# Which block of a feed-forward network goes through the down projection alone: the last instead of the first

## The chip, the core and the metric

The kernel runs on one core of a Trainium2 chip. The metric is device time in microseconds for the whole program, from one launch. Lower is better. The engines are called as in the profile: PE does the matrix products (PEld its weight loads), DVE elementwise work on two operands, ACT copies and activations, SP issues the loads.

## What is computed

Two token groups (512 and 256 rows of 1024 features) go through a trunk of two layers with shared weights, all in float32. Each layer is a half-weighted SwiGLU network, a mixer (gated and windowed attention in layer 0, neighbourhood attention in layer 1), and a second SwiGLU network. So there are four feed-forward networks ("networks 1 to 4" below), with a mixer between 1 and 2 and one between 3 and 4. The change touches these four alone:

```python
D_MODEL, D_FF = 1024, 2816

def swiglu(h, wg, wu, wd):
    return (jax.nn.silu(h @ wg) * (h @ wu)) @ wd

def odd_layer(x, f1_n, f1_g, f1_u, f1_d, mix_n, w_qkv, rpb, w_out, f2_n, f2_g, f2_u, f2_d):
    x = x + 0.5 * swiglu(rmsnorm(x, f1_n), f1_g, f1_u, f1_d)
    x = x + mixer_c(rmsnorm(x, mix_n), w_qkv, rpb, w_out)
    x = x + 0.5 * swiglu(rmsnorm(x, f2_n), f2_g, f2_u, f2_d)
    return x
```

## The kernel before

The activations lie transposed: features on the partitions, the 768 tokens of both groups along the row, cut into two halves of 384. Float32 is made from two parts of the type fp32r: every weight tile is split into a high part (`whi`, an ACT cast, L114) and the rest (`wlo`, a DVE subtraction, L115), every operand likewise (L196, L197), and one product is three matmuls of 128x384 (`mm3`, L176 to L181). The `w` pool has five buffers for `whi` and five for `wlo`, the `raw` pool four buffers of 512 KB for weights as they come from memory.

**A network** has 2816 = 11 x 256 hidden features, hence 11 "pairs" of 128-wide blocks, numbered 0 to 10. Gate, up and down projections of a pair are each a 2x2 block product that is done with seven products in place of eight, over sums and differences of the blocks. Sums of weights (`s1` to `s4`) are DVE operations at L609, 128x512 each; sums of operands are made once per network for the input (`b11`, `b21`, `t1`, `t2`, `t3`, `n4`, `b22`).

- *Pairs 0 to 3* are "early" (`EARLY = 4`). Their products with `b11` and `b21` are made ahead in the order `ORDER`, while the second token half is still being normalised. What is left of an early pair is p6, p7, p4, p5, p3 (L579): 5 products for gate and 5 for up, 120 matmuls. It begins with p6, whose weights are the sum `s2` times `t2`.
- *Pairs 4 to 9* run p1, p6, p2, p7, p5, p3, p4: 168 matmuls, and begin with p1, whose weights come straight from memory. Pair 10 has an order of its own that begins with p1 as well.
- `keep` (L494, ACT) copies a finished PSUM bank out as `u2` or `u3`, `add` (L499, DVE) adds the second product, `hidden` (L508 to L511) makes the scaled silu(gate) * up.
- While pair p runs, the operands of pair p-1's down projection are made (`operands`, 7 splits and 4 differences, 11 DVE operations). Of these the last six (`operands_2`) are put off into the following down projection where L445 says so.

**Down projections** of pairs 0 to 8 are made by `down` (L629), for two pairs at once or for one. It loads two rows of weights for each pair (L636), makes four sums for each, and runs seven products: 24 matmuls each for two pairs, 12 for one. Four PSUM banks a product are added to `acc` (tiles `p10` to `p13`) or into x by DVE (L661, four adds a product, five products); only in the call that holds pair 0 is `acc` copied by ACT (L659) and not added. ACT copies two sets of banks (L655). Pairs 9 and 10 are left to `down_last`; `last_operands` (L690) adds `acc` into x during pair 10.

PE runs in the order in which the program is written. The order on DVE, ACT and SP is chosen by the framework's list scheduler when the program is built, from priorities and from its own durations; buffers are given out by the same scheduler. On the chip each engine then takes its instructions in that fixed order, with semaphore waits.

In network 1, loads of the weights (L99) share SP's queue with 60 small transfers that build bias tables in memory (`skew`, L1402; `tab`, L1407), one after each weight load.

The calls of `down` are made in the loop at L587 to L593, which the change edits.

Of the kernel before, what the change touches and what calls it, by code (L numbers as in the profile page):

```python
# [20 lines left out]
NPAIR = FF // (2 * P)  # L21
# [30 lines left out]
class Trunk:  # L52
# [364 lines left out]
    def ffn(self, pre):  # L417
# [7 lines left out]
        acc = []  # L425
        d, dl = {}, {}

        def operands(q):


            h = hs.pop(q)
            sub = lambda o, x, y: nc.vector.tensor_tensor(out=o, in0=x, in1=y, op=ALU.subtract)
            d[q] = {}

            def put(n, src):
                d[q][n] = self.dtile(n), self.dtile(n)
                self.split(*d[q][n], src)

            h11, h12, h21, h22 = h[0, 0], h[0, 1], h[1, 0], h[1, 1]
            yield put("b11", h11)  # L440
            yield sub(h11, h12, h11)
            yield put("t1", h11)
            yield put("b21", h21)
            yield sub(h11, h22, h11)
            if q and q % 2 == 0:  # L445
                self.later = operands_2(h, sub, put)
                return
            for _ in operands_2(h, sub, put):
                yield

        def operands_2(h, sub, put):
            h11, h12, h21, h22 = h[0, 0], h[0, 1], h[1, 0], h[1, 1]
            yield put("t2", h11)
            yield sub(h12, h22, h12)
            yield put("t3", h12)
            yield put("b22", h22)
            yield sub(h21, h21, h11)
            yield put("n4", h21)

        def pair(p):  # L460
# [114 lines left out]
            if p:  # L575
                steps = operands(p - 1) if p < NPAIR - 1 else self.last_operands(dl, 0, hs[p - 1], acc)
# [10 lines left out]
        for p in range(NPAIR):  # L587
            for _ in stages[p]:
                pass
            if p == 1:  # L590
                acc += [self.fw.tile([P, H], F32, tag=f"p1{j}", name=f"p1{j}") for j in range(4)]
            if p % 2 and p < NPAIR - 1:
                self.down(pre, range(max(p - 2, 0), p), d, acc)  # L593
        kind = self.following[0]
        self.norm_begin(self.following)
        if kind == "f":
# [968 lines left out]
```

## Time and profile before

| what | us |
|---|---|
| median of three runs (2632.23 to 2636.09) | 2633.43 |
| the profiled execution, its own time | 2634.87 |
| its span, first to last instruction | 2633.1 |
| PE busy in it, 15094 matmuls | 2561.3 |
| DVE busy, 4793 instructions | 2267.8 |
| ACT busy, 2851 instructions | 1365.6 |

The mean granted clock of PE is 0.99. Three runs lie within 0.15% of each other. A busy PE says little by itself, because the matmuls overlap: one takes 0.33 us in the records and the next starts 0.17 us later. What counts is the start of one matmul against the start of the one before.

Where each network stands in the span, by the first matmul of pair 0's remaining products and the last of `down_last`: network 1 from 60.5 to 518.7, network 2 from 810.7 to 1267.2, network 3 from 1303.0 to 1759.4, network 4 from 2159.4 to 2617.5.

### The profile page before, as it was taken

Reading aid. Unit: us, or ns where it says so; the run is one execution under the profiler, and the core shown is the slowest. Engines: PE = TensorE matmul, PEld = TensorE weight load, DVE = VectorE, ACT = ScalarE, POOL = GpSimd, SP = SyncE. Lnnn points to the kernel's source line nnn. Section 1 sums busy time; section 2 is a strip of 40 time slices with the busy share of each in tenths; the row PEclk is TensorE's granted clock in tenths of the full one; section 3 lists DMA queues with packets and bytes.
Section 4 is the critical chain, followed back from the end, with each engine's and each line's share of the span. In section 5 each row is a group of like instructions: output and inputs, shape, how many; then the busy total and the mean of one; then the engine's idle time right before and its main releaser. Section 6 shows DMA issues by size and latency. Waiting matters only on the chain.

```text
span 2633.1 us, 41175 instructions
## 1 busy us (share of the span) xinstructions
PE 2561.3 (97%) x15094; PEld 2491.3 (95%) x15094; DVE 2267.8 (86%) x4793; ACT 1365.6 (52%) x2851; POOL 88.0 (3%) x172
## 2 busy tenths in 40 slices
PE   7999999998999999999999999999999999999997
PEld 7999999987899999999999999989998989999997
DVE  8998889889779988898999888886777699988886
ACT  7544444555655544454654544454545465454443
POOL 0000000000100000000000000001222100000000
PEclk9999999999999999999999999999999999999998
DMA  5423222421223222222322222232221332222221
GB/s 168 133 78 103 71 81 65 145 87 37 89 77 97 81 81 77 68 75 86 96 81 81 73 73 74 88 111 63 63 63 40 105 104 81 81 71 74 68 87 54
DMA packets 83898, 218.99 MB, mean 83 GB/s; under 512 B 20080, under 2 KB 32880, under 8 KB 83696
## 3 DMA queue, kind: packets, MB, share of 16 engines
q1 hardware_dynamic: 83552, 216.34, 26.5%
q8 instruction: 118, 1.93, 0.3%
q14 instruction: 84, 0.69, 0.1%
q10 hardware_dynamic: 144, 0.03, 0.0%
HBM read 206.90 MB, written 15.07 MB: 84 GB/s over the span
## 4 chain that ended last, share of the span: by engine, by line
PE 86%; DVE 9%; ACT 2%; DMA 2%; issue 1%; SPq 0%; DVEq 0%; ACTq 0%
PE ps_mm L140 54%; PE ps_aux L140 31%; DMA raw<-in_w 1%; DVE wlo L115 1%; PE ps_aux L144 1%; DVE s L609 1%; DVE xl L739 1%; ACT p L911 1%; DVE p L920 0%; DVE p L905 0%; DVE tl L197 0%; ACT whi L114 0%; ACT xh L738 0%; DVE ol L197 0%; DVE x L706 0%
## 5 line engine op out<-in xcount | busy, mean ns | idle before, releaser
L114 ACT CAST whi<-s 128x512 fp32r<-128x512 f32 x496 | 304.9, 621 | 390.6 <-DVE s L609 133.1
L114 ACT CAST whi<-raw 128x512 fp32r<-128x512 f32 x512 | 311.0, 619 | 257.8 <-PE ps_mm L140 116.8
L115 DVE TENSOR_TENSOR wlo<-s,whi 128x512 fp32r<-128x512 f32 x496 | 337.0, 685 | 61.1 <-ACT whi L114 60.8
L115 DVE TENSOR_TENSOR wlo<-raw,whi 128x512 fp32r<-128x512 f32 x494 | 337.5, 691 | 28.3 <-ACT whi L114 24.1
L140 PE MATMUL ps_aux<-dt,whi 128*128 128x384 f32 x864 | 219.3, 334 | 2.1 <-ACT whi L114 2.1
L140 PE MATMUL ps_mm<-db,whi 128*128 128x384 f32 x864 | 219.2, 334 | 0.0
L140 PEld LDWEIGHTS ps_aux<-dt,whi 128*128 128x128 f32 x864 | 156.0, 188 | 2.4 <-ACT whi L114 2.4
L140 PEld LDWEIGHTS ps_mm<-db,whi 128*128 128x128 f32 x864 | 156.1, 188 | 0.0
L140 PE MATMUL ps_mm<-xh,whi 128*128 128x512 f32 (+1 forms) x416 | 147.4, 354 | 3.8 <-ACT xh L738 3.8
L140 PE MATMUL ps_aux<-dt,wlo 128*128 128x384 f32 x432 | 144.4, 334 | 0.3 <-DVE wlo L115 0.3
L140 PE MATMUL ps_mm<-db,wlo 128*128 128x384 f32 x432 | 144.4, 334 | 0.0
L140 PE MATMUL ps_mm<-xl,whi 128*128 128x512 f32 (+1 forms) x416 | 142.3, 342 | 1.1 <-DVE xl L739 1.1
L140 PE MATMUL ps_mm<-xh,wlo 128*128 128x512 f32 (+1 forms) x416 | 142.1, 341 | 0.0
L609 DVE TENSOR_TENSOR s<-raw 128x512 f32<-128x512 f32 x124 | 85.0, 686 | 23.0 <-DMA raw<-in_w 22.9
L499 DVE TENSOR_TENSOR u<-ps_aux,u 128x384 f32<-128x384 f32 x176 | 97.0, 551 | 2.8 <-PE ps_aux L140 2.6
L609 DVE TENSOR_TENSOR s<-raw,raw 128x512 f32<-128x512 f32 x124 | 83.7, 686 | 18.2 <-DMA raw<-in_w 18.0
L140 PE MATMUL ps_aux<-dh,whi 128*128 128x384 f32 x384 | 97.6, 335 | 0.6 <-DVE x L706 0.6
L911 ACT ACTIVATE p<-p,st 128x256 f32<-128x256 f32 (+3 forms) x144 | 68.9, 480 | 55.0 <-DVE st L909 54.9
L494 ACT COPY u<-ps_mm 128x384 f32<-128x384 f32 x176 | 83.5, 474 | 24.2 <-PE ps_mm L140 24.0
L661 DVE TENSOR_TENSOR x<-ps_aux,x 128x384 f32<-128x384 f32 x160 | 86.0, 552 | 9.3 <-PE ps_aux L140 9.2
L140 PEld LDWEIGHTS ps_mm<-xh,whi 128*128 128x128 f32 x416 | 79.9, 192 | 14.1 <-ACT xh L738 4.9
L140 PE MATMUL ps_mm<-oh,whi 128*128 128x384 f32 x256 | 88.1, 344 | 4.6 <-DVE x L888 4.0
(486 smaller groups left out, 8058.2 us busy)
## 6 DMA issues: line engine op xcount, KB each, us to landing
raw<-in_w SPq DMA_DIRECT2D x350, 512.0 KB, 3.7
xdm<-x SPq DMA_DIRECT2D x16, 384.0 KB, 2.3
x<-in_x SPq DMA_DIRECT2D x16, 192.0 KB, 5.5
x<-xdm SPq DMA_DIRECT2D x8, 384.0 KB, 3.4
xold<-xdm SPq DMA_DIRECT2D x8, 384.0 KB, 3.0
out_y<-y SPq DMA_DIRECT2D x8, 384.0 KB, 2.4
tab<-skew SPq DMA_DIRECT2D x8, 256.0 KB, 4.8
raw<-in_w SPq DMA_DIRECT2D x8, 256.0 KB, 2.6
```

The costliest lines, as they stand in the source:

```text
L114: nc.scalar.copy(hi, src)
L115: (eng or nc.gpsimd).tensor_tensor(out=lo, in0=src, in1=hi.bitcast(F32), op=ALU.subtract)
L140: self.nc.tensor.matmul(out, lhsT=lhsT, rhs=rhs, start=start, stop=stop, **kw)
L144: self.nc.tensor.transpose(out, src, self.ident)
L494: nc.scalar.copy(e[n, out], bank[key, n])
L499: nc.vector.tensor_tensor(out=t, in0=bank[key, n], in1=t, op=ALU.add)
L609: f = lambda o, x, y, op: self.nc.vector.tensor_tensor(out=o, in0=x, in1=y, op=op)
L661: nc.vector.tensor_tensor(out=o, in0=ps, in1=o, op=ALU.add)
L739: nc.vector.scalar_tensor_tensor(out=lo, in0=src, scalar=gain, in1=hi.bitcast(F32), op0=ALU.mult, op1=ALU.subtract)
L911: nc.scalar.activation(outs[i], outs[i], AF.Exp, bias=nm[:, i : i + 1], accum_out=sm[:, i : i + 1])
```

## The change

Pairs 0 to 8 are nine, so one of them goes alone. Before, it was pair 0, right after pair 1; then (1,2) after pair 3, (3,4) after pair 5, (5,6) after 7 and (7,8) after 9. Now (0,1) goes after pair 2, (2,3) after 4, (4,5) after 6, (6,7) after 8, and pair 8 alone after pair 9, just before pair 10. The operands that are put off are those of the second pair of each two: before of pairs 2, 4, 6, 8, now of 1, 3, 5, 7.

```diff
@@ operands @@
             yield sub(h11, h22, h11)
-            if q and q % 2 == 0:
+            if q % 2:
                 self.later = operands_2(h, sub, put)
                 return
@@ ffn @@
-            if p == 1:
+            if p == 2:
                 acc += [self.fw.tile([P, H], F32, tag=f"p1{j}", name=f"p1{j}") for j in range(4)]
-            if p % 2 and p < NPAIR - 1:
-                self.down(pre, range(max(p - 2, 0), p), d, acc)
+            if p and p % 2 == 0 and p < NPAIR - 1:
+                self.down(pre, range(p - 2, p), d, acc)
+            if p == NPAIR - 2:
+                self.down(pre, range(p - 1, p), d, acc)
```

The numbers of matmuls, DVE and ACT data operations and loads are the same in both; the lines behind L593 move down by two (L661 becomes L663). In the two mixers the order on DVE and ACT is the same in both kernels. In the networks it is the same in long stretches, with another pair in the same place, and differs most at two places: where the single down projection was, and where it is now.

**ACT at the start of pair 2, network 1.** `whi` is the high part of a weight, `u2` the copy of a finished bank, `db`, `dt`, `dn` operands of the down projection. Before, behind the single down projection:

```order
L516 COPY ps_mm80_1359<-p1_515 128x384
L516 COPY ps_mm82_1387<-p1_537 128x384
L516 COPY ps_mm94_1609<-p1_568 128x384
L516 COPY ps_mm96_1637<-p1_589 128x384
L494 COPY u2_1381<-ps_mm80_1359 128x384
L196 CAST db11_1383<-sg_539 128x384
L114 CAST whi83_1393<-s2_1391 128x512
```

Now, right behind pair 1:

```order
L114 CAST whi58_1192<-s2_1190 128x512
L196 CAST dt3_1117<-u2_726 128x384
L196 CAST db22_1143<-u3_772 128x384
L196 CAST dn4_1170<-sg_842 128x384
L509 ACTIVATE u3_1007<-u3_1007 128x384
L114 CAST whi60_1220<-s2_1218 128x512
L509 ACTIVATE u2_958<-u2_958 128x384
L114 CAST whi61_1241<-s3_1239 128x512
L494 COPY u2_1208<-ps_mm57_1186 128x384
```

Before, the weights of the "up" product with `t2` (`whi83`) stand behind the copy of the finished "gate" product (`u2`); now the same weights (`whi60`) stand four places ahead of that copy.

**DVE at the same place.** Before, the sum `s2` for "up" of pair 2 (`s2_1391`) comes behind the last adds into x of the single down projection:

```order
L661 TENSOR_TENSOR x4_101<-ps_aux64_1220,x4_101 128x384
L661 TENSOR_TENSOR x5_102<-ps_aux66_1226,x5_102 128x384
L661 TENSOR_TENSOR x6_103<-ps_aux68_1232,x6_103 128x384
L661 TENSOR_TENSOR x7_104<-ps_aux70_1238,x7_104 128x384
L609 TENSOR_TENSOR s1_1389<-raw21_1356 128x512
L609 TENSOR_TENSOR s2_1363<-raw18_1347,s2_1363 128x512
L609 TENSOR_TENSOR s2_1391<-s1_1389,raw20_1353 128x512
L609 TENSOR_TENSOR s3_1412<-raw18_1347,raw19_1350 128x512
L197 TENSOR_TENSOR db11_1384<-sg_539,db11_1383 128x384
L115 TENSOR_TENSOR wlo83_1394<-s2_1391,whi83_1393 128x512
```

Now the first down projection is that of pairs 0 and 1, behind pair 2, and ahead of pair 3 DVE has:

```order
L663 TENSOR_TENSOR x3_100<-ps_mm94_1601,x3_100 128x384
L611 TENSOR_TENSOR s1_1764<-raw27_1731 128x512
L663 TENSOR_TENSOR x4_101<-ps_aux80_1485,x4_101 128x384
L611 TENSOR_TENSOR s2_1766<-s1_1764,raw26_1728 128x512
L663 TENSOR_TENSOR x5_102<-ps_aux82_1494,x5_102 128x384
L663 TENSOR_TENSOR x6_103<-ps_aux84_1503,x6_103 128x384
L115 TENSOR_TENSOR wlo104_1769<-s2_1766,whi104_1768 128x512
L663 TENSOR_TENSOR x7_104<-ps_aux86_1512,x7_104 128x384
```

The sum for "up" (`s2_1766`) stands between the adds of the last product and not behind them.

**DVE between the last `down` and pair 10, network 2.** Before, with pairs 7 and 8 in that call, the adds into x stand mixed with the weights (`wlo`) and sums (`s1`, `s2`, `s3`) of pair 10:

```order
L661 TENSOR_TENSOR x3_7712<-ps_mm921_13095,x3_7712 128x384
L115 TENSOR_TENSOR wlo932_13245<-raw170_13220,whi932_13244 128x512
L661 TENSOR_TENSOR x4_7718<-ps_aux907_12979,x4_7718 128x384
L115 TENSOR_TENSOR wlo934_13267<-s2_13264,whi934_13266 128x512
L661 TENSOR_TENSOR x5_7724<-ps_aux909_12988,x5_7724 128x384
L661 TENSOR_TENSOR x6_8190<-ps_aux911_12997,x6_8190 128x384
L609 TENSOR_TENSOR s1_13288<-raw171_13222 128x512
L661 TENSOR_TENSOR x7_8196<-ps_aux913_13006,x7_8196 128x384
L609 TENSOR_TENSOR s2_13290<-s1_13288,raw170_13220 128x512
L609 TENSOR_TENSOR s3_13349<-raw168_13216,raw169_13218 128x512
```

Now pair 8 alone is in that call. Ahead of its last adds stand the weights of pair 10's first product, `wlo929` for gate and `wlo932` for up:

```order
L115 TENSOR_TENSOR wlo926_13177<-s2_13055,whi926_13176 128x512
L115 TENSOR_TENSOR wlo927_13197<-raw167_13051,whi927_13196 128x512
L115 TENSOR_TENSOR wlo929_13226<-raw168_13216,whi929_13225 128x512
L115 TENSOR_TENSOR wlo932_13245<-raw170_13220,whi932_13244 128x512
L663 TENSOR_TENSOR x4_7718<-ps_aux912_13089,x4_7718 128x384
```

Eight adds later (x5 to x7, x0 to x3, and x4 once more) DVE has:

```order
L663 TENSOR_TENSOR x5_7724<-ps_aux914_13095,x5_7724 128x384
L663 TENSOR_TENSOR x6_8190<-ps_aux916_13101,x6_8190 128x384
L663 TENSOR_TENSOR x7_8196<-ps_aux918_13107,x7_8196 128x384
L611 TENSOR_TENSOR s2_13264<-s1_13262,raw168_13216 128x512
L611 TENSOR_TENSOR s1_13288<-raw171_13222 128x512
L692 TENSOR_TENSOR x0_7694<-x0_7694,p10_9713 128x384
L115 TENSOR_TENSOR wlo934_13267<-s2_13264,whi934_13266 128x512
L611 TENSOR_TENSOR s2_13290<-s1_13288,raw170_13220 128x512
L611 TENSOR_TENSOR s3_13349<-raw168_13216,raw169_13218 128x512
```

The twelve adds of pair 8's last three products follow each other, with no weight or sum between them; the sums for pair 10's second product (`s2`) come behind the last of them, the weights of its first product ahead of the first.

## The prediction

> **What bounds the kernel now.** First the page: engines and the chain of work that ended last.
>
> ```profile
> PE 2561.3 (97%) x15094; PEld 2491.3 (95%) x15094; DVE 2267.8 (86%) x4793; ACT 1365.6 (52%) x2851; POOL 88.0 (3%) x172
> ...
> PE 86%; DVE 9%; ACT 2%; DMA 2%; issue 1%; SPq 0%; DVEq 0%; ACTq 0%
> ```
>
> The end is set by PE. PE's work is the same in both kernels, so only the time in which PE stands still or runs slowly can change. Where is it? I cut the networks into stages, each from the first matmul of a pair or a down projection to the first of the next. First undisturbed stages: pair 9, the double down projection of pairs 7 and 8, and pair 10 of network 2 (columns: the stretch, its length, busy time of each engine, granted clock, DMA).
>
> ```profile
> core 0: us, PE busy (x) PEld busy (x) DVE busy (x) ACT busy (x) POOL busy (x), PEclk, DMA share, GB/s
> 1145.69:1174.81 29.12, 29.12 (x169) 29.12 (x169) 26.09 (x48) 13.86 (x29) 0.00 (x0) 1.00 0.24 73
> 1174.81:1203.93 29.12, 29.12 (x169) 29.12 (x169) 26.79 (x51) 12.85 (x26) 0.00 (x0) 1.00 0.24 73
> 1203.93:1233.05 29.12, 29.12 (x169) 29.12 (x169) 25.88 (x48) 17.43 (x34) 0.00 (x0) 1.00 0.41 128
> ```
>
> 168 matmuls take 29.12 us, 0.173 us each, without a gap; an early pair's 120 should then take 20.80, a single down projection's 84 14.56. Now the places that the change touches. Network 1: pair 1, single, pair 2, pair 3, and later the double of pairs 3 and 4. Network 2: single, pairs 2 and 3. Networks 3 and 4: single and pairs 2 and 3.
>
> ```profile
> 81.62:102.42 20.80, 20.80 (x121) 20.80 (x121) 20.62 (x40) 12.05 (x25) 0.00 (x0) 1.00 0.39 127
> 102.42:116.98 14.56, 14.56 (x85) 14.56 (x85) 14.41 (x28) 9.57 (x21) 0.00 (x0) 1.00 0.34 110
> 116.98:139.96 22.98, 21.37 (x122) 20.74 (x122) 22.52 (x42) 11.66 (x24) 0.00 (x0) 1.00 0.40 116
> 139.96:161.85 21.89, 21.08 (x122) 20.75 (x121) 21.43 (x41) 11.49 (x22) 0.00 (x0) 1.00 0.33 105
> 249.25:281.38 32.13, 29.68 (x169) 29.04 (x169) 27.68 (x51) 13.80 (x27) 0.00 (x0) 1.00 0.20 66
> ...
> 853.45:868.01 14.56, 14.56 (x86) 14.56 (x85) 14.53 (x29) 9.68 (x21) 0.00 (x0) 1.00 0.26 73
> 868.01:891.68 23.67, 21.58 (x121) 20.66 (x121) 23.12 (x43) 11.87 (x24) 0.00 (x0) 1.00 0.27 89
> 891.68:912.65 20.97, 20.97 (x121) 20.75 (x121) 20.12 (x38) 11.39 (x22) 0.00 (x0) 1.00 0.31 101
> ...
> 1346.82:1361.38 14.56, 14.56 (x85) 14.56 (x85) 13.04 (x26) 9.49 (x21) 0.00 (x0) 1.00 0.12 43
> 1361.38:1383.63 22.25, 21.59 (x121) 20.66 (x121) 21.93 (x42) 12.07 (x24) 0.00 (x0) 1.00 0.31 96
> 1383.63:1404.53 20.90, 20.90 (x122) 20.76 (x121) 20.35 (x39) 11.29 (x22) 0.00 (x0) 1.00 0.29 101
> ...
> 2201.31:2215.87 14.56, 14.56 (x85) 14.56 (x85) 14.36 (x28) 9.58 (x21) 0.00 (x0) 1.00 0.26 74
> 2215.87:2240.67 24.80, 23.18 (x121) 22.27 (x121) 23.20 (x43) 12.01 (x24) 0.00 (x0) 0.93 0.28 85
> 2240.67:2261.57 20.90, 20.90 (x121) 20.77 (x121) 20.25 (x39) 11.28 (x22) 0.00 (x0) 1.00 0.31 101
> ```
>
> The single down projection itself loses nothing; its DVE is full (14.41 of 14.56). The stage behind it, pair 2, loses in all four networks: 2.18, 2.87, 1.45 and 4.00 us over 20.80, together **10.5 us**. Why it loses is seen in network 1 on the timelines of DVE, ACT and PE (start, length, engine, line, what; in brackets the idle time before and what ended it).
>
> ```profile
> 115.62 2.12 DVE L661 TENSOR_TENSOR x<-ps_aux,x 128x384 f32<-128x384 f32 x4
> 117.66 0.68 DVE L609 TENSOR_TENSOR s<-raw 128x512 f32<-128x512 f32 x1
> ...
> 118.86 0.68 DVE L609 TENSOR_TENSOR s<-s,raw 128x512 f32<-128x512 f32 x1
> ...
> 119.26 0.48 ACT L494 COPY u<-ps_mm 128x384 f32<-128x384 f32 x1 [3.09 <-PE ps_mm L140]
> 119.64 0.51 ACT L196 CAST db<-sg 128x384 fp32r<-128x384 f32 x1
> 120.05 1.14 ACT L114 CAST whi<-s 128x512 fp32r<-128x512 f32 x2
> ...
> 120.72 0.44 PE L140 MATMUL ps_mm<-t20h,whi 128*128 128x384 f32 x1 [1.50 <-ACT whi L114]
> ```
>
> Pair 2 begins with p6, whose weights are the sum `s2`. DVE comes to the sum for "up" only behind the last adds into x, which wait for the single's last product; that gives 118.86. ACT stands on the copy of "gate" (idle 3.09 us, until PE has finished it), and the split `whi` is queued behind. So PE finishes "gate" with nothing to go on. Network 4 has the same wait, and it is dearer there:
>
> ```profile
> 2219.61 0.44 PE L140 MATMUL ps_mm<-t20h,whi 128*128 128x384 f32 x1 [1.50 <-ACT whi L114]
> ...
> 2220.34 0.65 PE L140 MATMUL ps_mm<-t20h,wlo 128*128 128x384 f32 x1
> 2220.79 0.52 PE L140 MATMUL ps_mm<-t21h,whi 128*128 128x384 f32 x1
> ...
> 2223.67 0.41 PE L140 MATMUL ps_mm<-t30h,whi 128*128 128x384 f32 x1
> ```
>
> From 2220.34 to 2223.67 ten matmuls take 3.33 us, in place of 1.73: PE runs at about half pace (0.93 granted over the stage). That is 1.6 of the 4.0 us.
>
> The Trainium skill, "TensorE: Matmul & The Clock Gate", section "Why this matters for your kernels", says that the clock drops after idle gaps of more than about 3 us between bursts. By that rule a wait of 1.50 us would not bring the slow stretch, it would have another cause and might stay, and the sum below would be 10.9 in place of 12.5. The trace agrees in half: of three waits of 1.50 us one is followed by it and two are not. I keep the row, since nothing else stands before that stretch.
>
> **The change part by part.** *The wait behind the single goes*, 10.5 us as above: pair 2 follows pair 1 directly. In the new order the split for "up" (`whi60`) stands four places ahead of the "gate" copy, and its sum comes before the last operands of pair 1 are done. Nothing else waits behind it, since pair 1 follows pair 0 in that way already and takes 20.80.
>
> *The wait in the double of pairs 3 and 4, network 1.* It loses 32.13 - 29.12 = **3.0 us**:
>
> ```profile
> 249.45 0.56 DVE L510 TENSOR_TENSOR v<-ps_mm,acc 128x384 f32<-128x384 f32 x1 [1.52 <-PE ps_mm L140]
> 250.11 0.56 DVE L511 SCALAR_TENSOR_TENSOR sg<-sg,v 128x384 f32<-128x384 f32 x1
> 250.59 0.68 DVE L609 TENSOR_TENSOR s<-raw,raw 128x512 f32<-128x512 f32 x1
> ...
> 252.05 0.62 PE L140 MATMUL ps_aux<-dt,whi 128*128 128x384 f32 x2 [2.12 <-ACT whi L114]
> ```
>
> The sum is queued behind `v`, which waits for the last product of pair 4; DVE's idle time ends with PE, not with a transfer. No other network has this. That double no longer exists; (2,3) and (4,5) stand in its place, and their first sums stand ahead of `v` as they do in networks 2 to 4.
>
> *What moves behind pair 2 and 3.* The double (0,1) is now followed by an early pair, which needs sums at once. Its `s2_1766` stands between the adds of the last product, so the sum and the split for "up" have the 2.08 us of "gate" and more. Pair 3's own losses (1.09, 0.17, 0.10, 0.10 = 1.5) I leave where they are. They are unexplained, so below I let them go or come once more: 1.5 either way.
>
> *The single at its new place.* All loads stay two rows a pair, and the rate is that of the neighbours. ACT's four copies of `acc` become four adds on DVE, and four adds on DVE elsewhere become copies. Their price:
>
> ```profile
> 859.08 1.94 DVE L661 TENSOR_TENSOR x<-ps_mm,x 128x384 f32<-128x384 f32 x4
> ```
>
> DVE was busy 13.04 to 14.53 us in the single; with 1.9 more it needs 15.0 to 16.5 us for 14.56 of PE: a debt of 0.4 to 1.9 us a network. Hidden or paid? The cover is the lead of the weights. ACT waits for PE to give up weight buffers, which means that they are full:
>
> ```profile
> L114 ACT CAST whi<-raw 128x512 fp32r<-128x512 f32 x512 | 311.0, 619 | 257.8 <-PE ps_mm L140 116.8
> ```
>
> Five buffers of 2.08 us each make up to 10 us of lead; pair 9 ahead of it has 3.0 us of idle DVE. I take 0, the bounds are 0 and 4 x 1.9 = 7.6 us. *Behind it* stands pair 10 and not an early pair, and this is the point of the whole change: it begins with p1, whose weights are split ahead of the adds:
>
> ```profile
> 1203.93 0.33 PE L140 MATMUL ps_mm<-b110h,whi 128*128 128x384 f32 x1
> ...
> 1208.09 0.33 PE L140 MATMUL ps_mm<-t20h,whi 128*128 128x384 f32 x1
> ```
>
> So PE has 4.16 us of work when the last add ends. DVE needs two sums at a pace of 0.60, an add of 0.47 and a split of 0.68 for the first `t2` weights: 2.4 us. The hole that cost pair 2 its 10.5 us is covered with 1.8 us to spare.
>
> *The sum.* 10.5 + 3.0 = 13.5 us; I take off 1.0 for small waits that come back, such as this one in pair 2 of network 2, which has nothing to do with the single:
>
> ```profile
> PE ps_aux L140 <- DVE u L499: 0.5, 1, 0.5
> ```
>
> That leaves 12.5 us: 2634.87 - 12.5 = 2622.4 for the profiled execution. Its own time is 1.44 above the median of the runs, so the median becomes 2633.43 - 12.5 = **2621**.
>
> **The rivals.** *The waits come back smaller.* Pairs 0, 1 and 2 now run without the single between them, DVE being at 20.62 of 20.80 in pair 1. If DVE is late there as in pair 3 of network 1 (1.09), each network pays about 1.1, and the gain is 13.5 - 4.4 - 1.0 = 8: 2625. Against it: pair 2 has five operand operations in place of eleven.
>
> *The 3.0 us stay*, because the table transfers of network 1 are what makes that double late, and they only meet another stage: 13.5 - 3.0 - 1.0 = 9.5, 2624. Against it stands the DVE row that ends with PE.
>
> *Nothing is won.* DVE's work is the same and the early stages are full; the 10.5 us are then paid by pair 3, behind the double, with its sums between the adds: 2633. Against it: a double leaves DVE 2 to 3 us free (26.79 of 29.12), the single none.
>
> *Slower.* In the single at its new place DVE's debt is not covered: PE loses 1.9 us there, and then as much as pair 2 lost (10.5 / 4 = 2.6) at pair 10's `t2`, with the half pace of network 4 (1.6) in each network, 6.1 us. Four times 6.1 less 13.5 is 11 us more: 2644. It decides from 3.4 us a network on (13.5 / 4), and counts as slower from 4.7. For it: pair 9 has all eleven operand operations of pair 8 ahead of the single, where six of them were put off before. Against it: 4.16 us of p1.
>
> **How the numbers follow.** A measurement of this kernel can tell about 0.2% (5.3 us) from no change. Forecast 2621: 0.60. Smaller waits, 2625: 0.15. The 3.0 stay, 2624: 0.08. Nothing won: 0.10. Slower: 0.07. Below 2628.2 lie the first three: faster 0.83, same 0.10, slower 0.07. Range: at the low end 13.5 and the 1.5 of pair 3 and a run's spread of about 1, 2617.5; at the high end 12.5 less 7.6 of debt gives 2628.5. The two left out are nothing won and slower.
>
> **What would show it.** Right: pair 2's stage takes 20.8 to 21.3 us in all four networks, no wait of 1.50 us on `whi` at its second product; the single between pairs 9 and 10 takes 14.56 and pair 10 29.12; doubles in network 1 all take 29.1. Wrong: pair 3 over 22 us (the wait has only moved), the new single over 15.5 or a wait at pair 10's `t2` (debt), or a stage in network 1 that ends its waiting with a transfer.

## The result, and the profile after

The changed kernel takes **2618.58 us** (median of five runs, 2616.48 to 2619.30), beside 2635.23 us for the kernel before in five runs next to it. The ratio is 0.9939, 95% interval 0.9927 to 0.9951: faster by 0.6%, or 16 us (13 to 19). A second set of five runs (e1) gave 2620.45 us and 0.9946 (0.9934 to 0.9959), 14 us. By the medians of the two sets alone the gain is 16.7 and 12.5 us. Forecast were 2621 us and 12.5 us. The profiled execution took 2616.48 us, its span 2614.7.

The page of the profile after, engines and the chain that ended last:

```profile
PE 2553.1 (98%) x15094; PEld 2488.8 (95%) x15094; DVE 2264.1 (87%) x4793; ACT 1366.3 (52%) x2851; POOL 88.4 (3%) x172
...
PE 88%; DVE 8%; ACT 2%; issue 1%; DMA 1%; SPq 0%; DVEq 0%; ACTq 0%
```

PE still sets the end. The stages of the changed kernel, cut as in the prediction. Network 1: pair 1, pair 2, double (0,1), pair 3, and the double (2,3); at its end the single and pair 10. Networks 2, 3 and 4: pair 2, the double (0,1), and in network 2 pair 3.

```profile
80.60:101.40 20.80, 20.80 (x122) 20.80 (x121) 20.77 (x41) 10.91 (x23) 0.00 (x0) 1.00 0.43 140
101.40:122.23 20.83, 20.83 (x121) 20.76 (x121) 18.88 (x35) 11.05 (x21) 0.00 (x0) 1.00 0.38 129
122.23:151.35 29.12, 29.12 (x169) 29.12 (x169) 26.84 (x50) 15.52 (x32) 0.00 (x0) 1.00 0.29 85
151.35:172.15 20.80, 20.80 (x121) 20.80 (x121) 20.70 (x40) 11.85 (x24) 0.00 (x0) 1.00 0.44 122
172.15:201.27 29.12, 29.12 (x169) 29.12 (x169) 27.29 (x49) 14.95 (x29) 0.00 (x0) 1.00 0.30 86
...
434.23:448.79 14.56, 14.56 (x85) 14.56 (x85) 14.24 (x29) 6.97 (x14) 0.00 (x0) 1.00 0.10 36
448.79:477.91 29.12, 29.12 (x169) 29.12 (x169) 27.37 (x52) 16.05 (x31) 0.00 (x0) 1.00 0.28 91
...
847.16:868.42 21.26, 21.11 (x122) 20.79 (x121) 20.19 (x37) 10.96 (x21) 0.00 (x0) 1.00 0.29 101
868.42:897.54 29.12, 29.12 (x170) 29.12 (x169) 26.02 (x49) 16.02 (x33) 0.00 (x0) 1.00 0.23 72
897.54:918.34 20.80, 20.80 (x122) 20.80 (x121) 20.54 (x40) 11.17 (x23) 0.00 (x0) 1.00 0.34 102
...
1336.30:1357.10 20.80, 20.80 (x122) 20.80 (x122) 19.76 (x37) 10.32 (x20) 0.00 (x0) 1.00 0.32 106
1357.10:1386.86 29.76, 29.39 (x170) 29.07 (x170) 25.36 (x48) 16.10 (x33) 0.00 (x0) 1.00 0.22 69
...
2186.86:2208.07 21.21, 21.07 (x121) 20.76 (x121) 20.48 (x38) 10.96 (x21) 0.00 (x0) 1.00 0.31 104
```

Pair 2 loses 0.03, 0.46, 0.00 and 0.41 us over its 20.80 in place of 2.18, 2.87, 1.45 and 4.00. Pair 3 loses nothing, nor does a double in network 1. The single takes 14.56 and pair 10 29.12. What is new is 0.64 us in the double (0,1) of network 3.

I take a stage's *loss* as its length less 0.1733 us for each of its matmuls (29.12 / 168). The table adds losses over the four networks, in one profiled execution of each kernel; "middle" is all from the end of pair 1 to the end of pair 3, "behind, network 1" is what lies behind that in network 1 (in the kernel before, almost all of it is the double (3,4)). Labels are those of the experiments below; the median is that of the kernel's own runs, the ratio is to runs of the kernel before on the same chip.

| kernel | pairs 0, 1 | middle | behind, network 1 | all | median us | ratio |
|---|---|---|---|---|---|---|
| before | 4.05 | 11.96 | 3.05 | 19.1 | 2633.43 | 1 |
| before again (e12) | 3.76 | 11.13 | 4.82 | 20.0 | 2632.76 | 1.0001 |
| changed | 2.52 | 1.54 | 0 | 4.1 | 2618.58 | 0.9939 |
| changed again (e1) | 4.55 | 1.47 | 0 | 6.0 | 2620.45 | 0.9946 |
| sums ahead (e2) | 3.85 | 9.94 | 5.48 | 19.4 | 2633.60 | 0.9999 |
| single before pair 3 (e3) | 2.38 | 18.05 | 0 | 20.4 | 2634.26 | 1.0005 |
| single behind pair 3 (e4) | 3.80 | 0.91 | 7.85 | 13.4 | 2625.66 | 0.9971 |
| changed, pair 1 not put off (e5) | 2.85 | 2.06 | 0 | 4.9 | 2619.91 | 0.9946 |
| lean pair 2 (e6) | 2.24 | 9.86 | 5.49 | 17.6 | 2634.08 | 0.9998 |
| lean and sums (e7) | 4.73 | 4.26 | 6.09 | 15.1 | 2628.43 | 0.9978 |
| single behind pair 5 (e8) | 2.93 | 0.73 | 0.28 | 3.9 | 2618.52 | 0.9941 |
| before, tables on GpSimd (e9) | 6.01 | 10.28 | 0.11 | 16.4 | 2631.66 | 0.9989 |
| lean, sums, tables (e10) | 4.30 | 3.56 | 0.14 | 8.9 | 2622.54 | 0.9959 |
| changed, tables on GpSimd (e11) | 6.35 | 0.87 | 0 | 7.2 | 2621.57 | 0.9953 |

From before to changed the losses fall by 15.1 us; 3.3 of the 18.4 us between the two profiled executions lie outside. Most of that is chance. The start of network 4, from its first product with `b11` to pair 0's remaining products, took 39.97 us in the first profile of before, and 39.0 us in the second profile of the changed kernel (e1). In the second profile of before, and in the first of the changed kernel:

```profile
2120.76:2158.18 37.42, 34.92 (x201) 34.23 (x201) 36.75 (x89) 28.48 (x59) 0.00 (x0) 1.00 0.38 127
```

```profile
2107.54:2144.91 37.37, 34.80 (x202) 34.21 (x201) 36.72 (x89) 28.39 (x59) 0.00 (x0) 1.00 0.40 128
```

### The profile page after: what moved, and what is told of

It reads as the page before. It is cut to its first block, busy times and chain, and to the rows that moved or that the text cites. A ratio compares the mean times of both kernels' runs of the same rounds, so it can differ in the third digit from the quotient of the medians.

```text
span 2614.7 us, 41195 instructions
## 1 busy us (share of the span) xinstructions
PE 2553.1 (98%) x15094; PEld 2488.8 (95%) x15094; DVE 2264.1 (87%) x4793; ACT 1366.3 (52%) x2851; POOL 88.4 (3%) x172
## 4 chain that ended last, share of the span: by engine, by line
PE 88%; DVE 8%; ACT 2%; issue 1%; DMA 1%; SPq 0%; DVEq 0%; ACTq 0%
PE ps_mm L140 55%; PE ps_aux L140 32%; DVE wlo L115 1%; PE ps_aux L144 1%; DMA raw<-in_w 1%; DVE xl L741 1%; ACT p L913 1%; DVE p L922 0%; DVE p L907 0%; DVE tl L197 0%; DVE tmp L362 0%; ACT xh L740 0%; DVE x L708 0%; DVE ol L197 0%; ACT whi L114 0%
## 5 line engine op out<-in xcount | busy, mean ns | idle before, releaser
L611 DVE TENSOR_TENSOR s<-raw,raw 128x512 f32<-128x512 f32 x124 | 84.0, 686 | 21.3 <-DMA raw<-in_w 21.1
L663 DVE TENSOR_TENSOR x<-ps_aux,x 128x384 f32<-128x384 f32 x160 | 84.9, 552 | 13.0 <-PE ps_aux L140 13.0
L663 DVE TENSOR_TENSOR x<-ps_mm,x 128x384 f32<-128x384 f32 x160 | 86.2, 551 | 5.8 <-PE ps_mm L140 5.4
```

The lines of the kernel that those rows point to most:

```text
L611: f = lambda o, x, y, op: self.nc.vector.tensor_tensor(out=o, in0=x, in1=y, op=op)
L663: nc.vector.tensor_tensor(out=o, in0=ps, in1=o, op=ALU.add)
```

## The experiments

**The theories.** The prediction said that the waits came from *order*: a few instructions in the fixed order of DVE and ACT stand badly behind the single, and with pair 1 ahead they stand well. The rival is *density*: with the single among the early pairs, DVE has more work in that stretch than PE has time, so PE must wait somewhere, whatever the order. The first shows in where a sum stands; the second in DVE's busy time over the whole stretch.

**e1, the changed kernel once more**, in the same set as e2 to e4.

> The changed kernel once more, as the mark for the three below. Both theories: ratio to before 0.993 to 0.995; its profile shows how far stages repeat. If the 2.6 us that network 4's start gained in the first profile (between its first b11 product and its first t2 product) and the 1.0 us that the mixer ahead of network 2 lost are chance, they take another value here, while pair 2 stays at 20.8 to 21.3 us in all four networks.

Measured: 2620.45 us, 0.9946 (0.9934 to 0.9959). The middle loses 1.47 us, as before 1.54. Pairs 0 and 1 lose 4.55 where they lost 2.52: so much differs from one execution to another there. Pair 2 takes up to 21.49 us (network 2), a little over the 21.3 that I expected.

**e2, the order alone.** The single stays first; the sums `s2` of pair 2 get the priority that those of pair 3 have. In the built order the sum then stands between the last four adds into x, and its split ahead of the copy of "gate".

```diff
-                    with self.tc.high_priority() if early and p == EARLY - 1 else nullcontext():
+                    with self.tc.high_priority() if early and p >= EARLY - 2 else nullcontext():
                         s2 = sums(n, "s2")
```

> The kernel before, with the first pair alone as it was; only the s2 sums of pair 2 get a higher priority. In the built order the sum for up then stands between the last four adds of the single down projection and not behind them, and its split ahead of the copy of the gate product. Same work, same place of the single. Theory 'order': the 10.5 us of pair 2 were made by those few instructions; pair 2's stage falls to 20.8 to 21.5 us in all networks, the 3.0 us in network 1's double of pairs 3 and 4 stay, the ratio is 0.996 to 0.9975 (8 to 10 us). Rival 'density': the early stages with the single among them hold as much DVE work as PE time, so the wait only moves to the next products (t3 of pair 2, pair 3), and pairs 2 and 3 together gain less than 4 us: ratio 0.9985 or more.

Measured: 2633.60 us, 0.9999 (0.9990 to 1.0008): no gain. The wait of 1.50 us is gone. Pairs 2 and 3 of network 1, and where PE waits in them (engine, what, line, the releaser, then us in total, times and the longest):

```profile
115.63:137.52 21.89, 21.21 (x121) 20.71 (x121) 21.63 (x41) 11.99 (x24) 0.00 (x0) 1.00 0.38 110
137.52:159.94 22.42, 21.35 (x122) 20.71 (x122) 22.25 (x43) 11.75 (x23) 0.00 (x0) 1.00 0.38 111
```

```profile
PE ps_mm L140 <- DVE wlo L115: 1.5, 2, 0.8
PE ps_mm L140 <- ACT whi L114: 0.3, 1, 0.3
```

Pair 2 loses 1.09 in place of 2.18 and pair 3 1.62 in place of 1.09, and DVE is busy for 21.63 of 21.89 and 22.25 of 22.42 us. PE now waits for the next things that DVE makes, `wlo`. Pairs 2 and 3 gain about 2 us in all, as the rival had it (under 4). So this order alone is not the cause; the first theory falls as it was stated.

**e3, the single before pair 3.** The single is (0) behind pair 2, and (1,2) follows pair 3. It is the kernel before with the single one place later, and one thing more: pair 1's last six operand operations are put off too, and the single makes them.

```diff
+DOWN = {2: (0,), 3: (1, 2), 5: (3, 4), 7: (5, 6), 9: (7, 8)}
...
-            if q and q % 2 == 0:
+            if q in (1, 2, 4, 6, 8):
...
-            if p % 2 and p < NPAIR - 1:
-                self.down(pre, range(max(p - 2, 0), p), d, acc)
+            if p in DOWN:
+                self.down(pre, DOWN[p], d, acc)
...
-            for _ in range(n if len(pairs) > 1 else 0):
+            for _ in range(n):
```

> Pair 0 alone, but behind pair 2, so that early pair 3, which begins with a sum, follows it; (1,2) after 3 and the rest as before. The operands of pair 1 are put off into the single as well, 6 DVE operations more in it. Theory 'order': the hole goes along with the single: pair 2 takes 20.8 to 21.3, pair 3 loses 1.5 to 4 us in each network, at its t2 or t3 product with a wait on whi or wlo; against the changed kernel 6 to 14 us more, ratio to before 0.997 to 1.001. Rival 'the end is what helps' (the gain comes from what the single does at the end of the network, or from pair 0 not being alone): also about 1.000, but the loss would not sit in pair 3.

Measured: 2634.26 us, 1.0005 (0.9997 to 1.0014). The loss went with the single: pair 2 loses at most 0.6 us, and the single and pair 3 pay. Network 4, both:

```profile
2222.66:2238.65 15.99, 15.23 (x86) 14.47 (x85) 15.43 (x31) 10.95 (x25) 0.00 (x0) 1.00 0.12 34
2238.65:2261.21 22.56, 21.37 (x122) 20.73 (x121) 22.33 (x43) 11.25 (x22) 0.00 (x0) 1.00 0.29 93
```

The put-off operands are made in the single here, so it holds 15.43 us of DVE work for 14.56 of PE, and no run says how much of this loss they make. The early pair behind it begins with p6, so it wants sums at once. Network 1 pays most, 2.61 us in the single and 6.07 in pair 3, more than the 4 that I gave as the most. The time is that of before all the same, because the double (3,4) of network 1 loses nothing in this kernel (see e9).

**e4, the single behind pair 3**, and so ahead of pair 4, which begins with p1: (0,1) behind pair 2, (2) behind 3, the rest as before.

```diff
+DOWN = {2: (0, 1), 3: (2,), 5: (3, 4), 7: (5, 6), 9: (7, 8)}
...
-            if q and q % 2 == 0:
+            if q in (1, 4, 6, 8):
...
```

> (0,1) after pair 2, then pair 2 alone after pair 3, then (3,4), (5,6), (7,8): the single stays next to the early stages but a pair that begins with p1 follows it. Theory 'order': p1 covers the sums, pair 4 behind the single takes 29.1 to 29.6, so the gain is there, but the built order of network 1 has the sum of the double (3,4) behind v again, as before: 3.0 us stay. Ratio 0.994 to 0.996. Rival 'density': the single still stands among full early stages and pairs 3 and 4 pay, half of the gain at most: 0.997 or more. Rival 'the end is what helps': 0.998 or more.

Measured: 2625.66 us, 0.9971 (0.9960 to 0.9981). In networks 2 to 4 the single takes 14.56 us and pair 4 loses 0.3. Network 2's single and pair 4, then network 1's double (3,4):

```profile
927.11:941.67 14.56, 14.56 (x86) 14.56 (x85) 14.42 (x29) 6.95 (x14) 0.00 (x0) 1.00 0.17 54
941.67:971.07 29.40, 29.40 (x170) 29.08 (x169) 28.34 (x53) 16.19 (x32) 0.00 (x0) 1.00 0.25 72
247.36:283.16 35.80, 32.48 (x170) 31.79 (x170) 28.29 (x51) 13.82 (x27) 0.00 (x0) 0.90 0.23 70
```

Nearly all that this version lacks against the changed kernel is network 1: pair 4 loses 1.18 and the double (3,4), which is behind pair 5 as it was before, 6.68 us. The ratio by itself lies where I had put the rival (0.997 or more); the rows speak against it, since the middle loses 0.91 us and pair 4 2.0 in the four networks together.

**e5, the changed kernel with pair 1's operands not put off.** In the program, six operand operations of DVE, about 2.8 us, go back from the double (0,1) to pair 2.

```diff
+        self.later = iter(())
...
-            if q % 2:
+            if q % 2 and q > 1:
                 self.later = operands_2(h, sub, put)
```

> The changed kernel with one thing undone: pair 1's last six operand operations on DVE (about 2.8 us of DVE in each network) are no longer put off into the double (0,1) but made in pair 2's stage, as the kernel before did. The single stays behind pair 9, the sum of work is the same, and no weight stands right ahead of its matmul in the built order. If the loss was DVE's density in the early stretch, pair 2 and the double behind it lose 0.5 to 2.5 us a network again: 2622 to 2629 us, ratio to before 0.996 to 0.9985. If it was the order of a few instructions alone, nothing comes back: 2618 to 2621 us, ratio 0.994 to 0.9955.

Measured: 2619.91 us, 0.9946 (0.9933 to 0.9960). Hardly anything comes back (the middle loses 2.06 us, against 1.54 and 1.47), as the order theory expected. But this tells nothing against density, because the scheduler left the operations where they were. Pair 2 of network 1:

```profile
100.83:121.64 20.81, 20.81 (x121) 20.75 (x121) 18.91 (x35) 10.97 (x21) 0.00 (x0) 1.00 0.39 127
```

DVE is busy for 18.91 us in it, against 18.88 in the changed kernel. In both, in all four networks, two splits of operands fall into pair 2 and five into the double (0,1).

**e6, less DVE work at pair 2.** The kernel before, with the single first; pair 1's last six operand operations are put off out of pair 2's stage into the double (1,2).

```diff
+            if q == 1:
+                self.late1 = operands_2(h, sub, put)
+                return
             if q and q % 2 == 0:
                 self.later = operands_2(h, sub, put)
+                if q == 2:
+                    self.later = self.both(self.late1, self.later)
                 return
...
+    def both(self, a, b):
+        for _ in a:
+            next(b, None)
+            yield
```

> The kernel before, single down projection still behind pair 1, but in each network six operand operations on DVE of pair 1 are put off from pair 2's stage into the double (1,2), which makes them in turn with those of pair 2. Same work, and the weights of the up product at pair 2 still stand behind the last adds into x. If density decides, pairs 2 and 3 together fall from the 11.8 us of before to 3 to 6 us over four networks: 2625 to 2629 us, ratio 0.997 to 0.9985. If the order of sum, copy and high part decides by itself, pair 2's waits stay near 1.5 to 2.9 us: 2631 to 2634 us, ratio 0.9992 to 1.0005.

Measured: 2634.08 us, 0.9998 (0.9989 to 1.0007). Pair 3's loss is gone in all four networks; pair 2's stays, at 2.17, 3.72, 1.80 and 2.17 us. PE at pair 2 of network 1:

```profile
120.35 0.44 PE L140 MATMUL ps_mm<-t20h,whi 128*128 128x384 f32 x1 [1.50 <-ACT whi L114]
```

The wait of 1.50 us on `whi` behind the copy of "gate" is the same to the hundredth. Less work alone isn't enough either.

**e7, both.** The edits of e2 and e6 together.

> Both edits in one: six operand operations of pair 1 put off out of pair 2's stage, and the sums s2 of pair 2 given the priority that lets them stand ahead of the last adds into x. The single stays behind pair 1. If the loss needs both (DVE too full, and an order that puts the lack at pair 2), pairs 2 and 3 lose under 2 us in four networks and what stays against the changed kernel is the 3 to 5.5 us in network 1's double (3,4): 2622 to 2626 us, ratio 0.9955 to 0.9975. If density alone decides, as e6 without these sums. If neither, as before, 2632 to 2634 us.

Measured: 2628.43 us, 0.9978 (0.9970 to 0.9987): faster by 5.8 us (3.4 to 7.9), a little less than the interval of ratios that I gave. The middle loses 4.26 us where I expected under 2, and network 1's double 6.09 where I expected 5.5 at most. Still, each edit alone left 9.9 us in the middle. So the waits at pairs 2 and 3 need both: an order that puts the lack in front of PE, and a DVE without the time to make it up. The single, pair 2 and pair 3 of network 1 as one stretch (56.16 us of matmuls) in before:

```profile
102.42:161.85 59.43, 57.01 (x326) 56.05 (x325) 58.37 (x109) 32.72 (x67) 0.00 (x0) 1.00 0.36 110
```

in e2 (order alone):

```profile
101.07:159.94 58.87, 57.12 (x326) 55.99 (x326) 58.20 (x110) 33.54 (x68) 0.00 (x0) 1.00 0.39 115
```

in e6 (less work alone):

```profile
102.05:160.38 58.33, 56.73 (x325) 56.09 (x325) 57.09 (x106) 31.89 (x65) 0.00 (x0) 1.00 0.39 116
```

in e7 (both):

```profile
100.61:157.88 57.27, 56.59 (x325) 56.09 (x325) 56.42 (x105) 31.98 (x64) 0.00 (x0) 1.00 0.40 118
```

and in the changed kernel, where the stretch is pair 2, the double (0,1) and pair 3 (70.72 us of matmuls):

```profile
101.40:172.15 70.75, 70.75 (x409) 70.68 (x409) 66.43 (x124) 38.42 (x77) 0.00 (x0) 1.00 0.36 109
```

Read DVE's busy time against the matmuls' time. Before and in e2, 58.4 and 58.2 us of DVE stand against 56.16: DVE is idle for about 1 us or less, PE has to wait for some 2 us in any order as long as this work falls into the stretch, and an earlier sum mostly makes another one late. In e6 DVE still has 57.1. In e7 it is down to 56.4 and the stretch to 57.27. In the changed kernel 66.4 stand against 70.7, and there are 4 us to spare.

The sum is a floor and not the whole loss. Networks 2 and 4 of before have 57.77 and 57.81 us of DVE, so the excess over 56.16 is 2.2, 1.6, 0 and 1.7 us in networks 1 to 4, 5.5 together, and the middle lost 12.0.

Network 3 is the exception. In before its stretch has less DVE work than PE work, and DVE waits there itself:

```profile
1346.82:1404.53 57.71, 57.05 (x326) 55.98 (x325) 55.32 (x105) 32.84 (x67) 0.00 (x0) 1.00 0.25 84
```

```profile
DVE s L609 <- DMA raw<-in_w: 1.1, 3, 0.5
DVE wlo L115 <- ACT whi L114: 1.0, 1, 1.0
```

55.32 us of work and 2.1 of waiting for weights and for `whi` make up the 57.71. It loses least, 1.55 us, and in e7 0.10. But a sum below the matmuls' time doesn't promise a stretch without loss. In e2 the same network lost 2.35 us, and in e9 (below) network 1 lost 1.82:

```profile
1347.20:1405.71 58.51, 57.09 (x326) 55.97 (x325) 56.00 (x106) 32.48 (x67) 0.00 (x0) 1.00 0.26 84
```

```profile
102.47:160.45 57.98, 57.25 (x326) 55.98 (x325) 54.98 (x104) 32.83 (x67) 0.00 (x0) 1.00 0.26 84
```

In both DVE waits for weights and for `whi` itself, 2.5 and 2.7 us. And a window counts what falls into it: DVE made 109 operations in network 1's stretch before and 104 in e9, for the same matmuls. So the table shows that both things matter together; how much of a loss is DVE's lack of time and how much its waiting stays open.

**e8, the single behind pair 5** (pair 4 alone), ahead of pair 6.

```diff
+DOWN = {2: (0, 1), 4: (2, 3), 5: (4,), 7: (5, 6), 9: (7, 8)}
...
-            if q and q % 2 == 0:
+            if q in (1, 3, 6, 8):
...
```

> The single down projection at pair 4, behind pair 5: (0,1) after pair 2, (2,3) after 4, 4 alone after 5, (5,6) after 7, (7,8) after 9. It stands far from the early pairs and is followed by pair 6, which begins with p1. If all that counts is that the single leaves the early stretch and that a pair with p1 follows it, the time is that of the changed kernel: 2618 to 2622 us, ratio 0.994 to 0.9957. If the place at the end brings something of its own (pair 10 takes the debt, down_last starts with less ahead of it), it is 2624 us or more, ratio 0.9965 and up.

Measured: 2618.52 us, 0.9941 (0.9928 to 0.9953), the same as the changed kernel. Network 1, the single and pair 6:

```profile
259.01:273.57 14.56, 14.56 (x85) 14.56 (x85) 14.56 (x29) 6.35 (x13) 0.00 (x0) 1.00 0.24 73
273.57:302.98 29.41, 29.41 (x170) 29.09 (x170) 28.25 (x53) 16.06 (x32) 0.00 (x0) 1.00 0.24 72
```

DVE is full in the single, and pair 6 loses only 0.29. The end of the network has no merit of its own; what counts is that the single isn't among the early pairs and that a pair with p1 follows it.

**e9, the double of network 1.** The kernel before, with the 60 table transfers issued by GpSimd and not between network 1's loads on SP. In the built order, the sum behind `v` in the double (3,4) and the split behind the copy at network 1's pair 2 are then gone.

```diff
-        dma = self.nc.sync.dma_start
+        dma = self.nc.gpsimd.dma_start
```

> The kernel before, with the 60 small transfers of the bias tables issued by GpSimd and no longer on SP's queue between network 1's loads. In the built order this takes away network 1's two tight places (the sum behind v in the double (3,4), and the high part behind the copy of gate at pair 2) and leaves those of networks 2 and 4 as they were. If network 1's double loses by that order, its 3.0 to 6.7 us go, pair 2 and 3 of network 1 still lose about 2 us together, since DVE's work in the early stretch is the same, and networks 2 to 4 are as before: 2626 to 2630 us, ratio 0.9968 to 0.9988. If the double waits for something else (a load, a bank), the wait stays and the time is 2632 us or more.

Measured: 2631.66 us, 0.9989 (0.9980 to 0.9998), just outside what I expected (up to 2630 us and 0.9988). The double runs without a wait:

```profile
247.91:277.04 29.13, 29.13 (x170) 29.13 (x170) 24.77 (x47) 12.80 (x26) 0.00 (x0) 1.00 0.25 73
```

Pairs 0 and 1 lose 6.01 us in this execution, against 3.8 to 4.1 in the two of before, which hides a part. Not all of that is chance: network 1's pair 1 loses 1.0 to 1.3 us in the three kernels with the transfers on GpSimd (e9, e10, e11), where DVE waits 1.2 to 1.9 us for weights, and nothing in the eleven other executions. Pair 2 of network 1 still loses 1.57, though its split now stands ahead of the copy.

The edit takes away both the order and the transfers. e3 parts them. Its transfers are on SP, its double (3,4) of network 1 stands behind pair 5 as before, the last two table transfers go out 8.4 and 7.8 us ahead of that double (8.5 and 7.9 before), and the last two weights land 7.4 and 4.7 us ahead of it (7.5 and 4.8 before). But in its order the first sum stands ahead of `v`. That double, from 254.37, takes 29.12 us:

```profile
251.47 0.69 DVE L610 TENSOR_TENSOR s<-raw,raw 128x512 f32<-128x512 f32 x1
...
254.81 0.55 DVE L511 TENSOR_TENSOR v<-ps_mm,acc 128x384 f32<-128x384 f32 x1
```

So the order is what costs there, and not the transfers.

**e10, all three**: the edits of e7 and e9, the single still behind pair 1.

> The single still behind pair 1 as before, with three edits in one: six of pair 1's operand operations put off out of pair 2's stage, pair 2's sums s2 ahead of the last adds into x, the tables' transfers on GpSimd. If the three account for the changed kernel's gain, what is left against it is the 1 to 1.5 us a network at pair 2 that the lean kernel with sums ahead still lost: 2621 to 2625 us, ratio 0.995 to 0.9968. If the gain comes from something else that the place of the single alone brings, it stays at 2627 us or more.

Measured: 2622.54 us, 0.9959 (0.9947 to 0.9972). Against e7 that is 5 us less by the ratios and 5.9 by the medians: about the loss of 6.09 in that double. The three edits bring the single at its old place to within 2 to 5 us of the changed kernel; the profile shows them as what pair 2 still loses in networks 2 and 4 (1.81 and 1.42) and 0.9 in a pair 4.

**e11, the changed kernel with the tables on GpSimd**, the control for e9.

> The changed kernel with the tables' transfers on GpSimd: the control for that edit by itself. The changed kernel has no tight place in network 1, so if the transfers matter through the order alone, nothing moves: 2617.5 to 2621 us, ratio 0.9938 to 0.9955. If they cost time on SP's queue by themselves, it is faster than the changed kernel by 1 us or more: 2615 to 2617.5 us.

Measured: 2621.57 us, 0.9953 (0.9940 to 0.9965): no gain, perhaps 1 to 2 us lost, which fits pairs 0 and 1 losing 6.35, 1.27 of it at network 1's pair 1. So moving the transfers off SP's queue gains the changed kernel nothing, and in the kernel before they cost through the order that the scheduler made with them.

**e12, the kernel before once more.**

> The kernel before once more, unchanged, for a second profile beside the first. If the losses come from the kernel and not from one execution, network 1's pairs 2 and 3 lose 3 us together again, networks 2 to 4 lose 2 to 4 us at pair 2, and what lies outside the networks' pairs (the start, the mixers) differs by 1 to 3 us. The double (3,4) of network 1 loses 3.0 us if that is its price in this kernel, 5 to 7 us if the first profile caught it low, as three kernels with the same order there suggest. Time 2631 to 2636 us, ratio 0.9992 to 1.0008.

Measured: 2632.76 us, 1.0001 (0.9992 to 1.0010). The middle loses 11.13 us, as before 11.96. The double of network 1, with 0.95 granted:

```profile
248.62:282.30 33.68, 31.24 (x170) 30.59 (x169) 27.94 (x51) 13.80 (x27) 0.00 (x0) 0.95 0.19 63
```

It takes 33.68 us here, so it loses 4.56, between the two values that I had expected, for the same wait of 2.12 us. The 5.48, 6.68, 5.49 and 6.09 us of e2, e4, e6 and e7 are no further draws of this: the order there is worse by a place, with the sum behind the split of `dt` too, and PE waits 2.76 us. In e2:

```profile
248.82 0.56 DVE L197 TENSOR_TENSOR dt<-sg,dt 128x384 fp32r<-128x384 f32 x1
249.29 0.69 DVE L609 TENSOR_TENSOR s<-raw,raw 128x512 f32<-128x512 f32 x1
```

In before the sum starts at 250.59 and `dt` at 251.19. Pair 2 loses 9.0 us in this execution, in place of 10.5.

## Why the prediction was right, and where it wasn't

**The wait behind the single goes, 10.5 us: right in size.** Pair 2 lost 10.5 us and loses 0.9. The split for "up" is made well ahead, three places before the copy of "gate" in ACT's order (and not four). What is tight now is the product after it, "gate" with `t3`. Network 1, pair 2 from 101.40, ACT, DVE and PE:

```profile
100.01 0.62 ACT L114 CAST whi<-s 128x512 fp32r<-128x512 f32 x1 [2.15 <-DVE s L611]
...
103.08 0.62 ACT L114 CAST whi<-s 128x512 fp32r<-128x512 f32 x1 [0.62 <-DVE s L611]
...
103.48 0.33 PE L140 MATMUL ps_mm<-t20h,whi 128*128 128x384 f32 x1
...
103.68 0.48 ACT L494 COPY u<-ps_mm 128x384 f32<-128x384 f32 x1
...
105.08 0.69 DVE L115 TENSOR_TENSOR wlo<-s,whi 128x512 fp32r<-128x512 f32 x1
...
105.56 0.33 PE L140 MATMUL ps_mm<-t30h,whi 128*128 128x384 f32 x1
```

The split of 100.01 is that for "up" and is done 2.9 us before PE wants it at 103.48. The split of 103.08 is that of `s3` for `t3`; its low part on DVE ends at 105.77, when PE is already in that product, and PE still goes on in its stride. In networks 2 and 4 this is where the 0.46 and 0.41 us are lost, in network 2 so:

```profile
851.99 0.44 PE L140 MATMUL ps_mm<-t30h,wlo 128*128 128x384 f32 x1 [0.15 <-DVE wlo L115]
```

The 10.5 us were themselves one draw. The slow stretch of 1.6 us in network 4 is missing in e12, where pair 2 lost 9.0; with the wait it went as well, so the sum of 10.9 us in which it stays fell too.

**The reason given for it was half of it.** The prediction named the order ("the split `whi` is queued behind"). It is needed, as e6 shows, but e2 took this place out of the order and gained nothing. The other half stood in the rows that the prediction quoted, and was not added up: DVE 14.41 + 22.52 + 21.43 = 58.4 us in three stages with 56.2 us of matmuls. The rival "nothing is won" rested on this very point ("the early stages are full") and was rightly set low, since a double leaves DVE free; that is the argument that should have carried the forecast. That the size came out although the reason was incomplete is luck in part: the change happens to cure both halves at once.

**Pair 3's 1.5 us, left as they were: wrong.** They went. They were unexplained in the prediction; e6 and e7, which took DVE work out and left pair 3 without a loss, show them as the tail of the same lack.

**The double of pairs 3 and 4: right in kind, its size a draw.** It was 3.0 in the sum and 3.0 between the two profiles. The kernel's second profile (e12) has 4.6, because a slow stretch follows the same wait there. With pair 2's 9.0 the two terms come to 13.6 in e12 and to 13.5 in the sum; that they agree is luck, since the one was high and the other low.

**What the forecast fell short by.** Of the 15.1 us between the two profiles, 9.6 are pair 2, 3.0 the double, 1.5 pair 3, and 1.5 pairs 0 and 1, where the changed kernel's own two profiles differ by 2.0; 0.6 are lost anew. Pair 3 is the part of the shortfall that the runs explain; the gain of 14 to 16 us by the ratios is too near to 12.5 to divide it further.

**The rival that the 3.0 us stay** fell: no double of network 1 loses anything in the changed kernel, with the transfers where they were.

**Small waits of 1.0: near**, at 0.9 in pair 2 and 0.64 in the double (0,1) of network 3, 1.5 together. The one that was named, 0.5 us on `u` in pair 2 of network 2, isn't among them. The rival "the waits come back smaller" (4.4 us) fell with these numbers. One ground was too wide: pair 1, said to take 20.80, took 21.61 in network 3 of the same profile (1325.21 to 1346.82).

**The single's debt at its new place, taken as 0: right**, but not by the cover that was named. DVE is busy for 14.24 of 14.56 us in the new single, so the 15.0 to 16.5 us that were worked out for it didn't come, and no run shows whether the lead of the weights would have hidden them. The margin at pair 10 was smaller than forecast. DVE and PE from the single's last adds on, network 1:

```profile
447.60 1.95 DVE L663 TENSOR_TENSOR x<-ps_aux,x 128x384 f32<-128x384 f32 x4
...
448.79 0.33 PE L140 MATMUL ps_mm<-b110h,whi 128*128 128x384 f32 x1
...
449.46 0.68 DVE L611 TENSOR_TENSOR s<-s,raw 128x512 f32<-128x512 f32 x1
...
450.06 0.69 DVE L611 TENSOR_TENSOR s<-raw 128x512 f32<-128x512 f32 x1
...
451.13 0.69 DVE L115 TENSOR_TENSOR wlo<-s,whi 128x512 fp32r<-128x512 f32 x1
...
452.95 0.33 PE L140 MATMUL ps_mm<-t20h,whi 128*128 128x384 f32 x1
```

The adds end 0.76 us into pair 10 (449.55 less 448.79), and the first `t2` weights are ready at 451.82, 3.0 us into it; PE wants them at 452.95. DVE's work for them is the 2.4 us of the forecast (449.46 to 451.82); what was left out is that the adds end after pair 10 has begun. So 1.1 us were to spare and not 1.8. The slower rival wanted a wait here in each network; there is none.

## What to carry to other kernels

Where a wait sits and whether it can be removed are two questions. Before an order is blamed, add up the busy time of the engine that is waited for over the whole stretch between two places where it has slack; where it exceeds the time of the bounding engine, a better order mostly moves the wait, and less work only helps where the order lets it. The sum is a floor: an engine that waits for its own inputs can make the other wait below it as well. A short stage with the fixed work of a long one (here the single, with as many adds into x as a double) belongs ahead of a stage that begins with work prepared long before. A loss read from one profiled execution should be taken as a range if a slow stretch can follow it, and the losses of other kernels are no draws of it unless the order at that place is the same.

## What the runs showed of the hardware

PE's pace behind a wait differs from one execution to the next for the same instructions. After the wait of 1.50 us at pair 2, some ten matmuls took 0.32 us each in place of 0.17 in 3 of 11 cases over four executions (before, e6, e9, e12). After the wait of 2.12 us in network 1's double it was one of two, with 1.00 granted over the stage in before and 0.95 in e12. After the waits of about 2.8 us (e2, e3, e4, e6, e7) it was five of five, and after the four of 1.0 to 1.1 us in e3 never. Length doesn't decide alone: before a product with `b11` at the start of network 4 PE stands idle for 2.3 to 3.0 us, and the slow stretch follows in 6 of 14 executions, after 2.38 us in e6 but not after 3.03 us in e11. At the start of network 1, with 3.4 to 4.0 us, it was 14 of 14.

The Trainium skill, "TensorE: Matmul & The Clock Gate", section "Why this matters for your kernels", puts the limit at idle gaps of more than about 3 us. The runs agree from 3.4 us on; below it they show the slow stretch after 1.50 us already, and near 3 us it comes and stays away.
